# Two numbers in a kernel's planner: how many buffers stay reserved for elder requests

## The chip, the cores and the metric

The kernel runs on one core of a Trainium2 chip. A core has a matrix engine (TensorE, in the profile PE, with PEld for its weight loads), a vector engine (VectorE, DVE), a scalar engine (ScalarE, ACT), a general engine (GpSimd, POOL) and a sync engine (SP), which here only starts DMA transfers. Each works through its own list of instructions in order, and they wait for each other through semaphores. Working data lies in SBUF; matmul results go to PSUM, which has eight banks. The metric is the device time of one execution in microseconds (us), lower is better.

## The reference

The reference is one decoder block on a sequence of 2048 tokens of width 1024, in float32: a normalisation, one wide projection, two token mixers side by side (a gated linear recurrence and a chunked matrix memory with four heads), a merge with gates, an output projection, and a second normalisation with a residual.

```python
xn = rms_norm(x, g_pre)
proj = jnp.einsum("bsd,de->bse", xn, w_in)
...
u = causal_dwconv(r_x, rg_conv_w, rg_conv_b)
h_r = rg_lru(u, headwise(u, rg_w_a) + rg_b_a, headwise(u, rg_w_x) + rg_b_x, rg_lambda)
y_r = (h_r * jax.nn.silu(r_z.astype(jnp.float32))).astype(dt)
...
h_m = mlstm_chunkwise(q, k, v, i_pre, logf).transpose(0, 2, 1, 3)
...
y_m = (h_m * jax.nn.silu(m_z.astype(jnp.float32))).astype(dt)
y = jax.nn.sigmoid(gate_r) * jnp.einsum("bsr,rd->bsd", y_r, w_branch_r) + \
    jax.nn.sigmoid(gate_m) * jnp.einsum("bsm,md->bsd", y_m, w_branch_m)
out = jnp.einsum("bsd,de->bse", y, w_out)
return x + rms_norm(out, g_post)
```

## The kernel before

**Tiling and stages.** The 2048 tokens are four blocks of 512, taken in two passes (`sb` 0 and 1) of two blocks each. A pass is a phase A (projections and the recurrence) and a phase B (matrix memory, branch products, output). Nearly every working tile is 128 x 512 float32. To keep float32 accuracy, each matmul operand is split into a rounded high part and a low rest (`split`, `wsplit`): a cast on ACT (or DVE) and a subtraction on DVE. Each product is then three matmuls: high x high, high x low, low x high.

**Phase A.** It starts with the normalised input. `build_first` makes the tiles `a11` and `a12` from the first block; `build_second` makes `s1`, `s2`, `s3`, `s4` and `a22` from both blocks, since the projection of two blocks is done with seven products in place of eight (class `Pair`). Both call `token_scale`, which loads the rows of a block (`xh`), sums their squares, forms the factor of each token (`rsm`, `rstd`), puts it on a diagonal (`dg`, two buffers), and spreads it with a matmul `ones x dg` into one PSUM bank, four times, once per 128 tokens; the bank is copied out as `rb`. Everything that `build_second` makes is scaled with `rb`. In program order phase A records four calls of `ogate(0, h)`, which need only `a11` and `a12` and take four PSUM banks each (512 tokens by 256 columns), and then `build_second`, recorded under `nc.urgent(SPRI)`. Then come the pairs with their convolutions, gates and scans, and four calls of `ogate(1, h)`.

**Phase B.** Eight heads, u = 0 to 7: four of the first block, four of the second. A head loads its tiles (`mxr`, `cs`, `th`, `mz`), computes values and queries (`v`, `q`), scores (`s1`, `s2`), and then four `chunk` steps; each takes one bank for its output (`pt`) and two for the state update (`pc`), the last chunk of all only the first. Matmuls of other work are recorded between the heads: the branch products of the recurrence while u < 4 (their 16 inputs `yr` are held as 32 slots), the branch products of the memory for the first block while u is 4 or 5 (they make the 16 parts of `y`), and for u = 6 and 7 one `out_half` each, 96 matmuls of 512 columns on `y` into four banks, recorded after the four chunks of that head. After u = 7 come the branch products of the second block, during which the next pass's `build_first` is recorded, and the second block's output.

**The planner.** Nothing is issued while this program runs. Each call is recorded as an operation with its engine, an estimated cost, a place in program order (`seq`) and a priority (`pr`): the place less what `nc.urgent(n)` grants. `nc.early(n)` moves weight loads and splits 200 places up. `Plan.order` then plays the program through in estimated time: whenever an engine is free, it takes the available operation of lowest `pr`, unless it lies over `AHEAD` = 600 places behind the oldest operation not yet placed, or `can` says no. Each engine's instruction list is the order found. Since that is so, in the profile nearly every instruction has line 200 (the helper that issues a recorded operation) or 235 (its alternative on the other engine): they are told apart by tiles.

**Buffers.** A ring is a set of equal buffers: 78 slots of 128 x 512 in SBUF (tag `t`), eight PSUM banks (tag `ps`), six raw weight buffers (`raw`), four each of `whi` and `wlo`, and small ones. A tile takes a buffer of its ring when its first operation is placed and gives it back after its last. Requests of one ring are sorted by the program order of that first operation. `can(op)` decides whether `op` may take its buffers now:

```python
elder, q = 0, r[2]
while r[1][q] is not b:
    elder += id(r[1][q]) not in given
    q += 1
if r[0] <= min(elder, KEEP.get(b.tag, elder)):
    return False
```

Here `r[0]` is the number of free buffers and `elder` the number of requests that stand before this one in program order and haven't been served. With an empty `KEEP` the test is `r[0] <= elder`: a request is refused unless, after every elder one has been served, a buffer would still be free. The priority plays no part in it.

Of the kernel before, what the change touches and what calls it, by code (L numbers as in the profile page):

```python
# [125 lines left out]
class Plan:  # L126
# [133 lines left out]
    def order(self):  # L260
# [23 lines left out]
        def can(op):  # L284
            for b in op.allocs:
# [4 lines left out]
# [5 lines that stand above are left out]
# [1075 lines left out]
SPARE = 0  # L1370
VB = 1
SB = {}
KEEP = {}
AHEAD = 600
RAWB = 6
WPRI = 200
# [80 lines left out]
```

## Time and profile before

| | us |
|---|---|
| median of the 3 runs | 2010.14 |
| lowest and highest | 2008.55 and 2012.41 |
| the profiled execution, its time | 2010.83 |
| the profiled execution, its span from first to last instruction | 2009.1 |
| PE busy in it | 1969.2 (98%) |
| DVE busy | 1597.7 (80%) |
| ACT busy | 1142.2 (57%) |
| POOL busy | 517.2 (26%) |
| mean DMA rate | 156 GB/s |

The profile is of one execution. Its busy times are unions of an engine's instructions; matmuls overlap in the engine's pipeline, and their ends are modelled, so their starts are the safer reading. "Idle before" is the time in which an engine had nothing running before an instruction, put down to whatever ended that wait last. The granted clock is the share of full speed at which PE was allowed to run. The chain is followed back from the last instruction, at each step to what released it. Where 16 equal DMA engines are busy, the DMA share is their mean.

### The profile page before, as it was taken

Reading aid. Unit: us, or ns where it says so; the run is one execution under the profiler, and the core shown is the slowest. Engines: PE = TensorE matmul, PEld = TensorE weight load, DVE = VectorE, ACT = ScalarE, POOL = GpSimd, SP = SyncE. Lnnn points to the kernel's source line nnn. Section 1 sums busy time; section 2 is a strip of 40 time slices with the busy share of each in tenths; the row PEclk is TensorE's granted clock in tenths of the full one; section 3 lists DMA queues with packets and bytes.
Section 4 is the critical chain, followed back from the end, with each engine's and each line's share of the span. In section 5 each row is a group of like instructions: output and inputs, shape, how many; then the busy total and the mean of one; then the engine's idle time right before and its main releaser. Section 6 shows DMA issues by size and latency. Waiting matters only on the chain.

```text
span 2009.1 us, 30231 instructions
## 1 busy us (share of the span) xinstructions
PE 1969.2 (98%) x10240; PEld 1685.6 (84%) x10240; DVE 1597.7 (80%) x3026; ACT 1142.2 (57%) x2110; POOL 517.2 (26%) x864
## 2 busy tenths in 40 slices
PE   8999999999999999999999999999999999999998
PEld 8788888888898888887897788888888988888886
DVE  5998786978867889987559878879788677899783
ACT  5585664857555545644346757557585554465441
POOL 2444342343312111102033343432343111110010
PEclk9999999999999999999999999999999999999999
DMA  7224243242486466557471242413326754655562
GB/s 247 88 75 156 85 157 111 79 142 77 148 288 210 165 206 207 190 175 251 148 247 64 74 147 79 149 67 126 116 84 225 265 168 151 227 189 201 177 204 85
DMA packets 160988, 313.80 MB, mean 156 GB/s; under 512 B 19744, under 2 KB 40480, under 8 KB 160832
## 3 DMA queue, kind: packets, MB, share of 16 engines
q1 hardware_dynamic: 133440, 223.53, 33.9%
q0 software_dynamic: 27104, 88.21, 11.3%
q8 instruction: 80, 1.31, 0.3%
q14 instruction: 76, 0.62, 0.1%
q10 hardware_dynamic: 288, 0.13, 0.0%
HBM read 226.82 MB, written 84.97 MB: 155 GB/s over the span
## 4 chain that ended last, share of the span: by engine, by line
PE 95%; DVE 3%; ACT 1%; DMA 1%; issue 0%; SPq 0%; POOLq 0%; POOL 0%; ACTq 0%; DVEq 0%
PE ps L200 95%; DVE wlo L200 0%; DMA xh<-in_x_dram 0%; DVE kl L200 0%; DVE ql L200 0%; DMA xr<-in_x_dram 0%; DVE q L200 0%; DVE a L200 0%; ACT whi L200 0%; DVE mbc L200 0%; DVE cst L200 0%; DVE yml L200 0%; DVE th L200 0%; DVE cs L200 0%; ACT mbc L200 0%
## 5 line engine op out<-in xcount | busy, mean ns | idle before, releaser
L200 ACT CAST whi<-raw 128x512 fp32r<-128x512 f32 (+1 forms) x515 | 319.0, 621 | 544.9 <-PE ps L200 447.8
L200 DVE TENSOR_TENSOR wlo<-raw,whi 128x512 fp32r<-128x512 f32 (+1 forms) x576 | 394.0, 686 | 180.0 <-ACT whi L200 170.5
L200 DVE SCALAR_TENSOR_TENSOR u<-xq,vecs,u 128x511 f32<-128x511 f32 (+2 forms) x192 | 142.8, 746 | 9.5 <-ACT u L200 8.0
L200 DVE TENSOR_TENSOR raw<-raw,raw 128x512 f32<-128x512 f32 (+1 forms) x208 | 142.3, 686 | 2.7 <-DMA raw<-in_w_mo_dram 0.9
L200 POOL TENSOR_SCALAR h<-halo,vecs 128x2 f32<-128x2 f32 (+1 forms) x128 | 107.5, 853 | 1.5
L200 PE MATMUL ps<-ymh,whi 128*128 128x512 f32 x256 | 98.8, 395 | 2.7 <-ACT ymh L200 2.0
L200 PE MATMUL ps<-yrh,whi 128*128 128x512 f32 x256 | 100.8, 395 | 0.0
L200 PE MATMUL ps<-yml,whi 128*128 128x512 f32 x256 | 100.1, 392 | 0.7 <-DVE yml L200 0.7
L200 PE MATMUL ps<-yrl,whi 128*128 128x512 f32 x256 | 100.2, 391 | 0.0
L200 PE MATMUL ps<-yrh,wlo 128*128 128x512 f32 x256 | 100.0, 391 | 0.0
L200 PE MATMUL ps<-ymh,wlo 128*128 128x512 f32 x256 | 99.8, 391 | 0.0
L200 ACT ACT_TABLE_LOAD x65 | 83.4, 1283 | 4.0 <-PEq L1445 1.7
L200 PE MATMUL ps<-s2h,whi 128*128 128x512 f32 x192 | 75.4, 393 | 6.0 <-ACT m L200 6.0
L200 POOL COPY halo<-xq 128x3 f32<-128x3 f32 x64 | 48.7, 761 | 122.3 <-DVE xq L200 117.4
L200 PE MATMUL ps<-a11h,whi 128*128 128x512 f32 x192 | 76.3, 397 | 1.1 <-ACT whi L200 1.1
L200 PE MATMUL ps<-a11h,wlo 128*128 128x512 f32 x192 | 75.7, 394 | 0.9 <-DVE wlo L200 0.9
L200 PE MATMUL ps<-whi,yh 128*128 128x512 f32 x192 | 75.0, 391 | 1.0 <-ACT dn L200 1.0
L200 PE MATMUL ps<-s3h,whi 128*128 128x512 f32 x192 | 75.1, 391 | 0.8 <-ACT v L200 0.8
L200 PE MATMUL ps<-a11l,whi 128*128 128x512 f32 x192 | 75.5, 393 | 0.0
L200 PE MATMUL ps<-s2h,wlo 128*128 128x512 f32 x192 | 75.4, 393 | 0.0
L200 PE MATMUL ps<-s2l,whi 128*128 128x512 f32 x192 | 75.2, 392 | 0.0
L200 PE MATMUL ps<-a12h,whi 128*128 128x512 f32 x192 | 74.9, 390 | 0.0
(327 smaller groups left out, 6405.5 us busy)
## 6 DMA issues: line engine op xcount, KB each, us to landing
raw<-in_w_ch_dram SPq DMA_DIRECT2D x288, 256.0 KB, 2.7
raw<-in_w_out_dram SPq DMA_DIRECT2D x64, 256.0 KB, 2.7
raw<-in_w_mo_dram SPq DMA_DIRECT2D x48, 256.0 KB, 5.7
xh<-in_x_dram SPq DMA_DIRECT2D x32, 256.0 KB, 5.3
dth<-th POOLq DMA_DIRECT2D x32, 256.0 KB, 3.7
dgr<-tg POOLq DMA_DIRECT2D x32, 256.0 KB, 3.0
dmx<-xq POOLq DMA_DIRECT2D x32, 256.0 KB, 2.5
dc<-u POOLq DMA_DIRECT2D x32, 256.0 KB, 2.5
```

Of the source, the lines that this page charges most:

```text
L200: getattr(eng.real, what)(*[real(v) for v in a], **{n: real(v) for n, v in kw.items()})
```

## The change

One constant of the planner changes. For PSUM banks the number of elder requests that must be provided for is capped at two, and for the 78 SBUF slots at ten: with at least three free banks, or at least eleven free slots, any request is granted, however many elder ones are still open. Where fewer elders are open than the cap, the test is as before. The other rings (`raw`, `whi`, `wlo` and the small ones) have no entry and keep the old test. The recorded program, its operations, priorities, engines' estimated costs and the look-ahead of 600 are the same; only the order in which operations are placed on the engines can differ, and with it which physical buffer a tile gets, and which of two engines takes a copy that may run on either.

```diff
 SPARE = 0
 VB = 1
 SB = {}
-KEEP = {}
+KEEP = {"ps": 2, "t": 10}
 AHEAD = 600
 RAWB = 6
 WPRI = 200
```

## The prediction

> **What bounds the kernel now.** I read the page's busy times first, then its chain that ended last.
>
> ```profile
> span 2009.1 us, 30231 instructions
> PE 1969.2 (98%) x10240; PEld 1685.6 (84%) x10240; DVE 1597.7 (80%) x3026; ACT 1142.2 (57%) x2110; POOL 517.2 (26%) x864
> ...
> PE 95%; DVE 3%; ACT 1%; DMA 1%; issue 0%; SPq 0%; POOLq 0%; POOL 0%; ACTq 0%; DVEq 0%
> ```
>
> TensorE (PE) is busy for 1969.2 of 2009.1 us and is 95% of the chain. The change alters no instruction's work, only the order, so what it can win is PE's idle time, 39.9 us in all, and the time that PE loses to a lower clock after it has idled. Where the idle time lies is read from the windows view: a stretch, its length, busy time (and count) of PE, PEld, DVE, ACT, POOL, then the granted clock, the DMA share and GB/s.
>
> ```profile
> 0.00:50.00 50.00, 43.05 (x307) 40.91 (x308) 27.12 (x72) 27.21 (x64) 13.67 (x29) 0.97 0.71 247
> 50.00:112.00 62.00, 56.93 (x302) 47.86 (x300) 58.35 (x99) 37.88 (x67) 31.71 (x26) 0.97 0.23 77
> 112.00:783.00 671.00, 671.00 (x3406) 572.86 (x3405) 543.06 (x1000) 406.48 (x715) 194.68 (x344) 1.00 0.44 153
> ...
> 839.00:855.00 16.00, 12.80 (x87) 10.92 (x87) 16.00 (x35) 9.71 (x23) 1.79 (x3) 1.00 0.68 220
> 855.00:889.00 34.00, 33.74 (x185) 28.94 (x184) 24.09 (x54) 15.61 (x36) 2.39 (x5) 1.00 0.50 172
> 889.00:898.00 9.00, 6.54 (x47) 5.90 (x47) 8.93 (x20) 5.94 (x13) 0.00 (x0) 1.00 0.84 281
> ...
> 937.00:945.00 8.00, 5.08 (x20) 3.14 (x19) 7.14 (x12) 5.24 (x9) 0.00 (x0) 1.00 0.46 158
> ...
> 1060.00:1112.00 52.00, 45.76 (x185) 35.78 (x184) 50.08 (x85) 32.63 (x55) 24.75 (x26) 0.93 0.18 61
> 1112.00:1832.00 720.00, 719.83 (x3711) 616.29 (x3710) 592.61 (x1114) 434.25 (x777) 195.94 (x342) 1.00 0.44 150
> 1832.00:1849.00 17.00, 14.06 (x86) 12.49 (x85) 17.00 (x34) 10.81 (x25) 2.15 (x5) 0.90 0.65 220
> ...
> 1883.00:1888.50 5.50, 4.65 (x27) 3.66 (x27) 5.50 (x12) 3.63 (x8) 0.00 (x0) 1.00 0.96 352
> ...
> 2000.90:2009.10 8.20, 0.00 (x0) 0.00 (x0) 2.31 (x4) 0.69 (x2) 1.13 (x2) 0.82 0.16 64
> ```
>
> Length less PE busy is the idle time. The two long stretches hold 0.0 and 0.17 us in 1391 us: there the order can only lose. The first 50 us (6.95) and the tail (8.20) wait for the first loads and the last output. What is left are two kinds of places. **Kind A**, the start of each phase A, 5.07 us in 50:112 and 6.24 in 1060:1112, with DVE busy 58.35 of 62 and 50.08 of 52. **Kind B**, the last two heads of each phase B: 3.20 (839:855), 2.46 (889:898), 2.94 (1832:1849) and 0.85 (1883:1888.5), 9.45 together, with DVE busy nearly all the time. And 2.92 in 937:945, between them. So PE idles where DVE is full; the question is whether DVE was idle before, or PE had other work that the planner withheld.
>
> **Kind A: the scaling matmul that waits for sixteen banks.** The timeline of the second site, then the start of the first:
>
> ```profile
> 1025.60 0.28 DVE L200 TENSOR_SCALAR dg<-ident,rstd 128x128 f32<-128x128 f32 x1
> ...
> 1027.97 0.21 DVE L200 TENSOR_SCALAR rsm<-ss 128x1 f32<-128x1 f32 x1 [0.82 <-ACT xh L200]
> ...
> 1046.90 0.61 PE L200 MATMUL ps<-dg,ones 128*128 128x128 f32 x4
> ...
> 1047.39 0.51 DVE L200 TENSOR_SCALAR dg<-ident,rstd 128x128 f32<-128x128 f32 x2 [0.39 <-PE ps L200]
> ...
> 1048.82 0.59 ACT L200 COPY rb<-ps 128x512 f32<-128x512 f32 x1 [0.18 <-PE ps L200]
> ...
> 1049.44 0.75 DVE L200 SCALAR_TENSOR_TENSOR a<-a,vecs,rb 128x512 f32<-128x512 f32 x1 [1.54 <-ACT rb L200]
> ```
> ```profile
> 30.68 0.30 DVE L200 TENSOR_SCALAR dg<-ident,rstd 128x128 f32<-128x128 f32 x1
> ...
> 51.66 0.51 DVE L200 TENSOR_SCALAR dg<-ident,rstd 128x128 f32<-128x128 f32 x2 [0.39 <-PE ps L200]
> ```
>
> `dg` is ready at 1025.60, but the matmul that reads it runs at 1046.90; `rb`, on which all of build_second hangs, comes at 1048.82. That matmul has the highest priority of all (`urgent(BPRI)`, 1000), its input is there, and PE runs younger-priority matmuls meanwhile. Only `can` refuses it: its bank comes, in program order, behind the 4 x 4 = 16 banks of four `ogate` calls, and the old rule demands more free banks than elders not yet served. The first site shows the same 21 us between the second dg (30.68) and the third (51.66). What DVE did in the gap, by groups of lines, busy, mean ns, idle before:
>
> ```profile
> L200 DVE TENSOR_TENSOR wlo<-raw,whi 128x512 fp32r<-128x512 f32 x7 | 4.8, 692 | 14.0 <-ACT whi L200 14.0
> ```
> ```profile
> L200 DVE TENSOR_TENSOR wlo<-raw,whi 128x512 fp32r<-128x512 f32 x9 | 6.2, 692 | 10.4 <-ACT whi L200 10.3
> ```
>
> From 1029 to 1046.9 DVE idles 14.0 us, from 32 to 51 10.4 us, just ahead of the stretches in which it is full. With the new rule 3 free banks suffice. One ogate holds 4 of 8; the one before is evacuated soon after its last matmul, so 3 are free at some point of each ogate. I put rb about 19 us earlier: last rsm at 1027.97, plus what lies between the dg at 1047.39 and rb's end at 1049.41, 2.0 us, so about 1030. build_second has 44 full-width DVE operations; the chain's spacing of 0.6 us makes that 27 us, and a half fits into 14.0. Its s2 split, the 24th, was late by this much:
>
> ```profile
> 76.35 0.50 PE L200 MATMUL ps<-s2h,whi 128*128 128x512 f32 x1 [3.00 <-ACT m L200]
> ...
> 78.03 0.63 PE L200 MATMUL ps<-s2h,whi 128*128 128x512 f32 x1
> 78.46 0.63 PE L200 MATMUL ps<-s2l,whi 128*128 128x512 f32 x1
> ```
> ```profile
> 1072.09 0.50 PE L200 MATMUL ps<-s2h,whi 128*128 128x512 f32 x1 [3.00 <-ACT m L200]
> ```
> ```profile
> PE ps L200 <- DVE ul L200: 2.4, 2, 1.4
> ```
>
> 24 x 0.6 = 14.4 us from 1030 has it done by about 1049 beside the weights, 20 us ahead of use. The two 3.00 us waits go, and so should the short ones behind them. The 2.4 us for `ul` are the recurrence's own chain (convolution, split, gate) and stay. Kind A: 5.07 + 6.24 - 2.4 = **8.9 us**; bounds 0 and 11.3.
>
> **Kind B: out_half behind the chunks' banks.**
>
> ```profile
> 838.79 0.68 DVE L200 TENSOR_TENSOR yl<-tgl,yh 128x512 fp32r<-128x512 f32 x1
> ...
> 841.36 1.29 DVE L200 TENSOR_TENSOR wlo<-raw,whi 128x512 fp32r<-128x512 f32 x2
> ```
> ```profile
> 846.49 0.39 PE L200 MATMUL ps<-vh,kh 128*128 128x258 f32 x1 [1.66 <-ACT kh L200]
> ...
> 855.00 0.28 PE L200 MATMUL ps<-vh,kl 128*128 128x258 f32 x1
> 855.12 0.49 PE L200 MATMUL ps<-whi,yh 128*128 128x512 f32 x1
> ```
> ```profile
> 891.86 0.39 PE L200 MATMUL ps<-vh,wth 128*128 128x258 f32 x1 [1.36 <-ACT wth L200]
> ...
> 897.26 0.28 PE L200 MATMUL ps<-vh,kl 128*128 128x258 f32 x1
> 897.38 0.39 PE L200 MATMUL ps<-whi,yh 128*128 128x512 f32 x1
> ```
>
> The last part of y is split at 839.5 and two weights by 842.6, yet out_half starts at 855.12, straight behind the last of the four chunks' bank requests (12: one `pt` and two `pc` each), and again at 897.38. Between, PE waits for DVE with 96 ready matmuls of about 0.23 us (855.12 to 855.45 and on) withheld. The new rule lets out_half take banks down to two, and its matmuls fill the waits; DVE has 10 us free in 855:889 for what it then still owes. I take two thirds of 9.45, **6.3 us**, since a list made ahead won't meet every short wait; bounds 0 and 9.45.
>
> **The clock.** After the wait of 3.00 us the matmuls come 0.43 us apart (78.03 to 78.46), not 0.23. Granted clock times busy time gives 0.03 x 56.93 + 0.07 x 45.76 + 0.10 x 14.06 = 6.3 us lost in the three disturbed stretches. Half, **3.1 us**, should go with the waits. The Trainium skill, page "TensorE: Matmul & The Clock Gate", section "HAM oscillation — how this bites in real kernels", gives the rule "no PE-idle gaps >~3.4µs". By it gaps of 3.00 us and less would cost no clock, this term were 0 and the sum 3.1 us higher; the rows here show the slow matmuls all the same, so I keep it.
>
> **Slots.** With `"t": 10` a younger request needs at most 11 free of 78. It lets loads and splits run earlier: the 2.92 us of 937:945 might shrink (0 to 2.9; I take 0). Against it, younger tiles can eat what an elder head needs at once: eb, four k, two wt, four q halves, 11 slots, over the ten kept. Each DMA moved earlier also sits on SP ahead of weight loads behind it. The nearest row for such a stall is the 1.36 us wait above. Two of them are **2.7 us** lost; the far ends are none, and one in each of 16 heads, 22 us.
>
> **Sum.** 8.9 + 6.3 + 3.1 - 2.7 = 15.6 us. The profiled execution took 2010.83 us (span 2009.1 and 1.7 around it), 0.7 over the median of the three runs. 2010.8 - 15.6 gives 1995.2; I say **1995 us**. The bounds of its terms: everything goes and nothing is lost, 11.3 + 9.45 + 6.3 + 2.9 = 30, 1981; kind A alone, less the two stalls, 6, 2005.
>
> **Rivals.**
> 1. *Half of it.* DVE's 1597.7 us stay, and its queue is only shifted: the waits come back at the next needy place (gates, 937:945). For it speaks that DVE is 81% busy even in the long stretch (543.06 of 671); against it the 14.0 and 10.4 us of measured idle time. Half of 15.6: 2003 us. Chance 0.15.
> 2. *Nothing moves.* Another limit holds the same operations: the look-ahead of 600 (AHEAD), or the rings of weights, which keep the old rule. For out_half the weights are in place; the dg matmuls stand behind four ogates of 114 recorded operations and some 30 more, about 490, within the 600. So mostly against: 2010 us. Chance 0.11.
> 3. *Slower: slots run short in phase B.* While u < 4 the 32 slots of yr are held all along, and the early loads of the next head go in as soon as 11 are free. If a head then finds its eleven tiles one short, PE stalls by about 1.36 us per head; it decides against the change from about 13 heads on (13 x 1.36 = 18 against 18.3 won). With nearly all of 16 and kind B's gain lost too, 2010.8 - 12 + 22 = 2021 us. For it speaks that the two long stretches are full now and have nothing to win; against it that elder requests still go first whenever they are ready, and DVE has a fifth free. Chance 0.17.
> 4. *Slower by the clock.* If banks taken early leave PE many short idles, the granted clock of the long stretches could fall from 1.00 to the 0.97 seen in 50:112: 0.03 x 1391 = 42 us, 2036 us with the gains. No idle time there supports it. Chance 0.02. The Trainium skill's same page, section "A second HAM failure mode: psum-queue depth-cycling", tells of such oscillation; the trace shows none here.
>
> **How the numbers follow.** The forecast has 0.55, with its own range 1983 to 2004. Faster by over 0.2% (4 us, about what a measurement of this kernel tells from no change): forecast and rival 1, 0.70. Same: rival 2, 0.11. Slower: rivals 3 and 4, 0.19. Cases of one sign hold most, so there is one range, 1982 to 2013: it leaves out a little below, and most of rivals 3 and 4, some 0.18 in all.
>
> **What would show it.** Right: in the new trace the second pair of dg follows the first within some 5 us at both sites; rb near 34 and 1030; the DVE gaps filled; no 3.00 us wait before s2h; `ps<-whi,yh` starts before the head's last `vh,kh`, and the granted clock of 1060:1112 near 1.00. Wrong: dg still 20 us apart; out_half still behind the chunks; or PE idle time in the long stretches, ended by tiles that DVE or ACT wrote late, or by `tgl`, `cs` or `mxr` loads.

## The result, and the profile after

| | before | after |
|---|---|---|
| median, us | 2009.35 (2008.53 to 2012.41) | 1977.06 (1975.61 to 1977.79) |
| profiled execution, its time | 2010.83 | 1975.61 |
| its span | 2009.1 | 1973.8 |

The ratio is 0.9836, with a 95% interval of 0.9819 to 0.9853: 32.3 us faster. The forecast was 1995 us, with a range from 1982: the direction was right, the size was not, and the time lies below the range. The page of the changed kernel, span, busy times and the chain that ended last by engine:

```profile
span 1973.8 us, 30190 instructions
...
PE 1955.6 (99%) x10240; PEld 1679.8 (85%) x10240; DVE 1600.5 (81%) x3052; ACT 1158.6 (59%) x2108; POOL 551.0 (28%) x864
...
PE 96%; DVE 1%; POOL 1%; DMA 1%; issue 1%; ACT 0%; SPq 0%; POOLq 0%; ACTq 0%; DVEq 0%
```

PE issues the same 10240 matmuls. Its idle time fell from 39.9 to 18.2 us, but its **busy** time fell too, from 1969.2 to 1955.6, though no matmul went away. Of the 35.3 us that the span lost, 13.6 lay where the page says busy. The windows view (stretch, length, then busy time and count of PE, PEld, DVE, ACT, POOL, granted clock, DMA share, GB/s) answers to the stretches shown of before; all of phase B lies some us earlier now:

```profile
50.00:112.00 62.00, 60.89 (x325) 52.36 (x324) 56.96 (x104) 41.67 (x70) 36.70 (x37) 1.00 0.25 88
112.00:783.00 671.00, 671.00 (x3416) 572.76 (x3415) 542.19 (x1007) 406.58 (x712) 201.54 (x333) 1.00 0.44 154
820.00:860.00 40.00, 40.00 (x239) 35.34 (x238) 38.46 (x91) 23.47 (x49) 3.18 (x8) 1.00 0.58 188
860.00:900.00 40.00, 39.62 (x232) 34.47 (x231) 34.41 (x84) 22.89 (x56) 6.21 (x8) 1.00 0.88 307
900.00:945.00 45.00, 44.06 (x197) 35.85 (x197) 42.09 (x71) 21.09 (x40) 8.06 (x14) 1.00 0.63 212
1040.00:1092.00 52.00, 51.55 (x242) 42.97 (x241) 49.03 (x84) 36.29 (x57) 36.91 (x32) 1.00 0.20 71
1092.00:1790.00 698.00, 698.00 (x3592) 596.95 (x3592) 574.32 (x1083) 430.94 (x753) 202.91 (x338) 1.00 0.44 153
1790.00:1840.00 50.00, 50.00 (x290) 43.82 (x289) 46.47 (x108) 29.17 (x65) 4.87 (x9) 1.00 0.65 222
1840.00:1900.00 60.00, 59.52 (x314) 50.49 (x313) 44.20 (x91) 24.15 (x51) 10.28 (x17) 1.00 0.57 195
```

The two long stretches are as full as before (671.00 of 671.00 and 698.00 of 698.00), and no stretch here has a clock under 1.00. The places of kind A idle 1.11 and 0.45 us, those of kind B under half a us each. Who PE still waits for, in total, times, longest:

```profile
PE ps L200 <- DMA ident<-in_ident_dram: 3.9, 1, 3.9
PE ps L200 <- ACT uh L200: 1.6, 2, 1.1
```

and the same list of before, four rows that have no successor:

```profile
PE ps L200 <- ACT m L200: 6.0, 2, 3.0
...
PE ps L200 <- ACT kh L200: 4.0, 2, 2.4
...
PE ps L200 <- ACT ymh L200: 2.0, 1, 2.0
...
PE ps L200 <- ACT wth L200: 1.8, 3, 1.4
```

`ident`, the first load, leads now, and `uh`, the recurrence's own chain, is the longest wait in mid-kernel. The steps, in the timeline (start, duration, engine, operation, idle before it):

```profile
32.18 0.28 DVE L200 TENSOR_SCALAR dg<-ident,rstd 128x128 f32<-128x128 f32 x1
32.70 0.29 DVE L200 TENSOR_SCALAR dg<-ident,rstd 128x128 f32<-128x128 f32 x1 [0.24 <-POOL rstd L200]
...
34.12 0.59 ACT L200 COPY rb<-ps 128x512 f32<-128x512 f32 x1 [1.14 <-PE ps L200]
...
72.47 0.39 PE L200 MATMUL ps<-s2h,whi 128*128 128x512 f32 x1
...
837.19 0.47 PE L200 MATMUL ps<-whi,yh 128*128 128x512 f32 x1
...
1008.31 0.28 DVE L200 TENSOR_SCALAR dg<-ident,rstd 128x128 f32<-128x128 f32 x1
...
1011.48 0.29 DVE L200 TENSOR_SCALAR dg<-ident,rstd 128x128 f32<-128x128 f32 x1 [0.58 <-POOL rstd L200]
...
1012.81 0.32 DVE L200 TENSOR_SCALAR dg<-ident,rstd 128x128 f32<-128x128 f32 x1
...
1051.63 0.39 PE L200 MATMUL ps<-s2h,whi 128*128 128x512 f32 x1
```

The third and fourth `dg` stand within 3 us of the second (29.92) at the first site and within 5 us at the other. `rb` comes at 34.1 and, in the second pass, at 1014.2, which is 19 and 35 us earlier than before; of the 35, 17 come from the `dg` before it, which is itself that much earlier. In the gap, 32 to 51 us, DVE is now busy for 18.36 us (8.18 before). The first `s2h` matmuls (72.47, 1051.63) have no wait before them, and out_half starts at 837.19, ahead of that head's last `ps<-vh,kh` (851.41). Every step that was named as a sign is there. So the question is one of size.

**A finer measure.** Where a matmul waits, the modelled end of the one before it (0.39 us long, 0.23 apart) hides part of the wait, and half clock counts as busy. So for the table below each distance between the starts of two successive matmuls has the median distance of its shape before taken off (0.227 us at 512 columns, 0.120 at 256 and 258). What is left, summed, is **lost PE time**: 57.9 us before and 22.9 after, which is 35.1 less before rounding, against 35.3 of the span. By places: **A**, 50 to 150 and 1050 to 1150 us; **B**, 800 to 900 and 1750 to 1950; and **hand-over**, 900 to 950, where the last `ym` of a pass are loaded and split and the next input is made (the 937:945 of the prediction). The rest, 13 to 17 us, is much the same in all kernels. The places are read from one execution of each kernel, whose time lies within 1.7 us of the median, in e4 3.0 us below it.

| kernel | median, us | ratio, 95% interval | A | B | hand-over |
|---|---|---|---|---|---|
| before | 2009.35 | | 18.8 | 20.4 | 4.2 |
| after | 1977.06 | 0.9819 to 0.9853 | 2.1 | 4.0 | 1.5 |
| e3, scaling bank alone | 1992.54 | 0.9901 to 0.9930 | 1.1 | 20.9 | 3.1 |
| e4, out_half's banks alone | 2001.26 | 0.9942 to 0.9971 | 15.9 | 4.2 | 11.8 |
| e5, these five banks | 1984.68 | 0.9860 to 0.9889 | 1.9 | 3.5 | 10.1 |
| e1, all banks, no slots | 1985.16 | 0.9863 to 0.9896 | 3.3 | 3.5 | 10.6 |
| e2, slots, no banks | 1996.86 | 0.9924 to 0.9954 | 10.7 | 16.7 | 2.0 |
| e6, all but the scaling bank | 1985.28 | 0.9858 to 0.9891 | 10.5 | 4.8 | 1.5 |
| e7, all but out_half's banks | 1990.27 | 0.9882 to 0.9912 | 2.5 | 16.6 | 2.1 |
| e11, three banks kept back | 1977.84 | 0.9821 to 0.9851 | 2.6 | 7.2 | 0.9 |
| e8, four banks kept back | 1982.11 | 0.9842 to 0.9871 | 0.7 | 10.0 | 1.4 |
| e12, twenty slots kept back | 1986.74 | 0.9862 to 0.9895 | 2.7 | 4.2 | 10.7 |
| e13, banks, and slots for build_first | 1976.53 | 0.9821 to 0.9851 | 3.1 | 6.1 | 1.2 |
| e14, all but build_first's slots | 1979.36 | 0.9834 to 0.9863 | 2.2 | 3.1 | 4.9 |
| e18, e1 with build_first earlier | 1984.10 | 0.9858 to 0.9891 | 3.5 | 3.5 | 8.0 |
| e17, e1 with build_first later | 1982.63 | 0.9855 to 0.9884 | 2.7 | 4.0 | 7.8 |

### The profile page after: what moved, and what is told of

The parts are those of the page before. It is cut to its first block, busy times and chain, and to the rows that moved or that the text cites. A ratio compares the mean times of both kernels' runs of the same rounds, so it can differ in the third digit from the quotient of the medians.

```text
span 1973.8 us, 30190 instructions
## 1 busy us (share of the span) xinstructions
PE 1955.6 (99%) x10240; PEld 1679.8 (85%) x10240; DVE 1600.5 (81%) x3052; ACT 1158.6 (59%) x2108; POOL 551.0 (28%) x864
## 3 DMA queue, kind: packets, MB, share of 16 engines
q1 hardware_dynamic: 133440, 223.53, 34.1%
## 4 chain that ended last, share of the span: by engine, by line
PE 96%; DVE 1%; POOL 1%; DMA 1%; issue 1%; ACT 0%; SPq 0%; POOLq 0%; ACTq 0%; DVEq 0%
PE ps L200 96%; POOL hc L200 1%; DVE wlo L200 0%; DMA xh<-in_x_dram 0%; DMA dth<-th 0%; DMA gp<-in_gpost_dram 0%; DVE o L200 0%; DVE u L200 0%; DMA dym<-mz 0%; DVE th L200 0%; POOL out_dram L200 0%; POOL rstd L200 0%; POOL r L200 0%; DVE a22l L200 0%; ACT uh L200 0%
## 5 line engine op out<-in xcount | busy, mean ns | idle before, releaser
L200 ACT CAST whi<-raw 128x512 fp32r<-128x512 f32 (+1 forms) x484 | 300.2, 621 | 469.7 <-PE ps L200 367.0
L200 POOL TENSOR_SCALAR hc<-halo,vecs 128x3 f32<-128x3 f32 x64 | 81.6, 1275 | 8.1 <-DVE u L200 6.0
L200 POOL TENSOR_TENSOR rstd<-rsm,eps_t 128x1 f32<-128x1 f32 x32 | 20.2, 634 | 200.8 <-DVE rsm L200 186.1
L200 PE MATMUL ps<-wlo,yh 128*128 128x512 f32 x192 | 75.1, 391 | 0.0
L200 PE MATMUL ps<-whi,yl 128*128 128x512 f32 x192 | 74.9, 391 | 0.0
L200 PE MATMUL ps<-s3h,wlo 128*128 128x512 f32 x192 | 74.7, 389 | 0.0
```

What stands on the lines that cost most here:

```text
L200: getattr(eng.real, what)(*[real(v) for v in a], **{n: real(v) for n, v in kw.items()})
```

## The experiments

**The two numbers apart (e1, e2).**

```diff
-KEEP = {}
+KEEP = {"ps": 2}      # e1
+KEEP = {"t": 10}      # e2
```

> Only the bank half of the change: KEEP = {"ps": 2}, slots as before. Theory (the banks carry the gain): 1975 to 1982 us, no half-clock window after the first 50 us, PE idle time 18 to 21 us. Rival (the slots carry a good part, since loads and splits for the next head and the next input can start earlier): 1985 us or more, with the wait at 937 to 945 of the kernel before still there.

> Only the slot half: KEEP = {"t": 10}, banks as before. Theory: 2004 to 2012 us, the second pair of dg still some 20 us behind the first at both starts of a phase A, out_half still behind the chunks. Rival (slots carry a good part): 1990 to 2000 us. The prediction's third rival (slots run short in phase B): over 2013 us, with PE waits inside the long stretches.

Banks alone win 24.6 us, slots alone 12.9, both 32.3. That the slots win anything was against the forecast. They win at different places: with the banks alone A and B are cured and the hand-over gets worse, from 4.2 to 10.6; with the slots alone the hand-over is cured, A halved, and B barely touched. How the slots halve A stays open: in e2 `rb` comes as late as before (52.63 and 1042.36) and DVE is as idle from 32 to 51 us (8.74 us busy), yet both waits of 3.0 us for `m` are gone. PE's waits in e1, first row:

```profile
PE ps L200 <- ACT ymh L200: 5.8, 1, 5.8
```

**The banks, one request at a time (e3, e4, e5).** One buffer can be given a cap of its own, while all others keep the old test:

```diff
-                if r[0] <= min(elder, KEEP.get(b.tag, elder)):
+                if r[0] <= min(elder, KEEP.get(b.tag, elder) if b.keep is None else b.keep):
...
-        ps = psum()                         # token_scale, e3 and e5
+        ps = psum(2)
...
-        pt = [psum() for _ in range(NT)]    # out_half, e4 and e5
+        pt = [psum(2) for _ in range(NT)]
```

> KEEP is empty, and only the bank of token_scale is granted with three free banks: kind A of the prediction alone. The starts of the matmuls say that PE lost about 16.7 us more at the two kind A places before than after (distances between starts less the usual distance of each shape). Theory (the loss is to be read from matmul starts, and all of it goes): 1990 to 1995 us. Rival (the prediction's sizes, 8.9 us of idle time and some 2 of clock): 1997 to 2001 us. If kind A isn't held by that one bank: 2009 us.

> KEEP is empty, and only the four banks of each out_half are granted with three free banks: kind B of the prediction alone. Theory: 1990 to 1998 us, the waits in the last two heads of both phases B gone; the wait at 937 to 945 may stay, as it comes after out_half. Rival (the prediction's size, 6.3 us and some clock): 2001 to 2004 us. If out_half isn't held by its banks: 2009 us.

> KEEP is empty; the bank of token_scale and the four banks of out_half are granted with three free banks, all other banks as before. Theory (these five banks are the whole of the bank half): the time of the bank half alone, 1983 to 1987 us, which is also what the two single parts add up to (2009.8 - 17.2 - 8.5 = 1984). Rival (other banks, such as those of the pairs or the chunks, gain too): clearly above, 1989 us or more.

The edit stands in the two helpers, so it holds for every call: build_first's scaling matmul has the cap too, and so has the second block's out_half. The one bank of the scaling matmul wins 17.2 us. In the windows of e3 both places of kind A are at full clock, the first is full, and the second idles 1.01 us:

```profile
50.00:112.00 62.00, 62.00 (x333) 53.87 (x332) 55.79 (x99) 42.53 (x75) 35.88 (x36) 1.00 0.25 85
...
1040.00:1092.00 52.00, 50.99 (x275) 44.07 (x275) 47.11 (x79) 31.76 (x59) 33.38 (x26) 1.00 0.26 84
```

out_half's four banks win 8.5 by themselves, and 16.2 us of lost time at B, half of which is given back at the hand-over. (That 16.2 less 7.6 comes out near 8.5 is partly luck: the profiled execution was 12.6 us faster than that of before, 3 us of it at A, and it lacks two of the half-clock stretches of before, near 16 and 1108 us.) (In the kernels with a cap per buffer line 200 has become 201, and 235 has become 236.) PE's waits in e4, and what DVE does meanwhile:

```profile
PE ps L201 <- DVE ymh L236: 8.1, 1, 8.1
```
```profile
927.89 2.08 DVE L201 SCALAR_TENSOR_TENSOR a<-a,vecs,rb 128x512 f32<-128x512 f32 x3
929.88 1.89 DVE L201 TENSOR_TENSOR a11l<-a,a11h 128x512 fp32r<-128x512 f32 x3
931.68 2.07 DVE L201 SCALAR_TENSOR_TENSOR a<-a,vecs,rb 128x512 f32<-128x512 f32 x3
933.67 0.69 DVE L201 TENSOR_TENSOR a11l<-a,a11h 128x512 fp32r<-128x512 f32 x1
934.27 1.29 DVE L201 TENSOR_TENSOR a12l<-a,a12h 128x512 fp32r<-128x512 f32 x2
935.48 1.41 DVE L201 SCALAR_TENSOR_TENSOR a<-a,vecs,rb 128x512 f32<-128x512 f32 x2
936.80 0.42 DVE L236 CAST ymh<-ym 128x512 fp32r<-128x512 f32 x1
```

The next pass's input (`a`, `a11l`, `a12l`) fills DVE without a break from 927.9, and the cast of `ym` that PE stands still for comes behind it, in the order of the list; both last loads of `ym` had landed by 932.2. Both edits together (e5) give 25.2 us, about their sum of 25.7, and the time of e1: these five banks are the whole of the banks' half.

**Undoing one of them in the full change (e6, e7).** The same edit, the other way round: `psum(99)` in one place, so that this request alone keeps the old test.

> The changed kernel with the bank of token_scale alone under the old rule (more free banks than elders), all else as changed. Theory: kind A comes back as far as the slot half doesn't cover it; in the slot half alone the matmul starts show 5.4 + 5.4 us lost at the two places against 1.5 + 0.6 after the change, so 8 to 11 us more than the changed kernel, 1985 to 1988 us. Rival (with earlier slots the bank no longer matters): 1977 us.

> The whole change, but the four banks of out_half keep the old test. Theory (these banks are what freed the places of kind B): the matmuls of out_half come again behind the chunks' banks. With the slots alone the matmul starts of 800 to 850 us and of 1800 to 1850 us still lost 5.1 us each, so about 10 us come back: 1985 to 1989 us. Rival (the slots alone would have filled DVE in time, so the banks don't matter any more once they are there): 1977 to 1980 us, and out_half starts late without PE waiting.

Without the scaling bank 8.2 us come back, without out_half's banks 13.2. A comes back only by half (10.5 of 18.8): the slots alone had halved it too. B comes back for the most part (16.6 of 20.4), and out_half starts at 850.6 instead of 837.2; the time lies 1.3 us above the expected span.

**How many to keep back (e8, e11, e12).** `KEEP` with `"ps"` 4 or 3, or with `"t"` 20.

> Banks kept back: four in place of two; slots as in the change. Theory: an ogate holds four of the eight banks nearly all the time, so five free banks hardly occur while ogates run, the scaling matmul is refused as under the old test, and the second pair of dg comes near 51 and 1035 us again: about the 8 us of the run without that bank's grant, 1984 to 1988 us (a little more if out_half is refused too). Rival (any cap is enough, since five banks are free for a moment between two ogates): 1977 to 1979 us, dg near 30 us.

> Banks kept back: three in place of two. Theory: four free banks do occur beside an ogate that holds four, once the one before it is evacuated, so the scaling matmul is granted somewhat later than with two (dg and rb by a few us) and the time is that of the change, 1976 to 1980 us. Rival (the four are never all free while ogates run): as with four kept back, 1984 to 1988 us.

> Slots kept back: twenty in place of ten; banks as in the change. Theory 1 (the slots' part needs only that some loads of the hand-over go earlier, for which 21 free of 78 are enough part of the time): 1977 to 1980 us. Theory 2 (the slots are nearly all taken there, and each ten kept back delays the next input's loads): between the change and the banks alone, 1980 to 1985 us, with the first xh load of the second pass later than 870 us and a longer wait for ymh near 930 us.

Three is as good as two. Four costs 5 us, and not where it was expected: five banks are free often enough for the scaling matmul. Timeline of e8:

```profile
31.75 0.30 DVE L200 TENSOR_SCALAR dg<-ident,rstd 128x128 f32<-128x128 f32 x1
...
34.01 0.28 DVE L200 TENSOR_SCALAR dg<-ident,rstd 128x128 f32<-128x128 f32 x1
```

The loss is at B (10.0). out_half's first matmul comes as early as in the change (835.20), but its matmuls break off and go on at 848.96, and the chunks' matmuls between have waits again. That out_half asks for four banks in a row and gets the later ones late is the likely reason; no run tested it. Twenty slots lose the whole gain of the slots, with a wait of 5.75 us for `ymh` as in e1; the time lies 1.7 us above the expected span.

**Where the slots win (e13, e14, e18, e17).** In e13 the cap of ten slots holds only for the tiles made in build_first, in e14 for all but these. In e18 and e17 build_first is recorded elsewhere and the slots keep the old test.

```diff
+        v.buf.keep = slots[0]      # in t2k; slots[0] is set only inside build_first
...
-KEEP = {}
+KEEP = {"ps": 2}               # e13, slots[0] = 10
+KEEP = {"ps": 2, "t": 10}      # e14, slots[0] = 999
...
-XAT = 2
+XAT = 0                        # e18, with KEEP = {"ps": 2}
+XAT = 5                        # e17, with KEEP = {"ps": 2}
```

> The bank half (KEEP = {"ps": 2}), and the slot cap of ten only for the tiles made inside build_first (xh, rb, the a tiles and their splits). Theory (what the slots win on top of the banks is the next pass's input, whose 24 DVE operations stand in front of the last ym splits in the two bank-only kernels): 1976 to 1979 us, the wait before the first matmul on the last ymh, 5.8 us in the bank half alone, under 1 us. Rival (heads' loads or others carry it): 1983 to 1986 us.

> The changed kernel with the tiles made inside build_first under the old slot rule. Theory: 1983 to 1987 us, as the bank half alone, with a wait of some 5 us before the matmul on the last ymh. Rival (heads' loads or others carry the slots' part): 1976 to 1979 us.

> The banks' half of the change alone (slots under the old test), and the next input's build_first recorded two branch products earlier in program order (XAT 0 in place of 2). Theory (what the slots bought is that the next input's loads and its rb come earlier, so that build_first's DVE operations no longer stand between rb and the last splits of ym): fewer elder requests stand before it, its xh loads move up under the old test too, rb comes before 915 us (922.2 with the banks alone), PE's wait for ymh falls from 5.8 to under 3 us and the half clock behind it goes: 1976 to 1981 us. Rival (the slots helped somewhere else, and the hand-over only shows it): the wait may shift, but the time stays at 1984 to 1987 us.

> The banks' half alone, and build_first recorded three branch products later (XAT 5 in place of 2). Theory: rb comes no earlier than 922 us, and 13 of build_first's DVE operations in place of 15 still stand ahead of the last yml in DVE's list, so the wait for ymh stays near 5 us: 1983 to 1987 us. Rival (recording it later puts the splits of ym first and is as good as giving it slots early): 1976 to 1981 us with a wait under 3 us.

build_first's slots suffice (1976.5), but are hardly needed: the 1979.4 of e14 lie under what was expected of it. And an early `rb` is not what counts: in e18 it comes at 906.0 instead of 922.2, but the time stays at 1984, as the rival had it, with 4.4 us of waiting for `ymh`. Recorded later (e17), the time is 1982.6, 0.4 us under what the theory gave, with waits of up to 3.1 us in place of one near 5. The timeline of e18 shows why, DVE first, then ACT:

```profile
917.40 1.41 DVE L200 SCALAR_TENSOR_TENSOR o<-o,rstd,xr 128x512 f32<-128x512 f32 x2
...
919.92 2.07 DVE L200 SCALAR_TENSOR_TENSOR a<-a,vecs,rb 128x512 f32<-128x512 f32 x3
921.91 1.89 DVE L200 TENSOR_TENSOR a11l<-a,a11h 128x512 fp32r<-128x512 f32 x3
...
924.32 2.07 DVE L200 SCALAR_TENSOR_TENSOR a<-a,vecs,rb 128x512 f32<-128x512 f32 x3
926.31 1.89 DVE L200 TENSOR_TENSOR a12l<-a,a12h 128x512 fp32r<-128x512 f32 x3
928.12 0.74 DVE L200 SCALAR_TENSOR_TENSOR a<-a,vecs,rb 128x512 f32<-128x512 f32 x1
...
930.15 1.29 DVE L200 TENSOR_TENSOR yml<-ym,ymh 128x512 fp32r<-128x512 f32 x2
```
```profile
928.89 0.62 ACT L200 CAST a12h<-a 128x512 fp32r<-128x512 f32 x1 [1.85 <-DVE a L200]
929.42 1.14 ACT L200 CAST ymh<-ym 128x512 fp32r<-128x512 f32 x2
```

PE waits for the cast `ymh`, here on ACT. It stands in ACT's list behind casts of `a`, and these wait for DVE. With an early `rb` (e18) 15 of build_first's 16 operations of `a`, `a11l` and `a12l` stand between the last output operation (`o`) and the last split of `ym`, without it (e1) all 16.

Part of such a wait is the load of `ym` itself, which is issued late. In e1 the earlier of the last two loads lands at 924.64, half a microsecond after PE fell idle, and its cast starts at 929.22, so some 4.6 of the 5.8 us are the order of the lists. In e17 that load takes 8.4 us, lands at 926.21, and is cast at 927.08: there half of the longest wait of 3.1 us is the load.

In the changed kernel half of the 16 have gone ahead of the output operations. Two rows from either side of those, same view:

```profile
900.41 2.08 DVE L200 SCALAR_TENSOR_TENSOR a<-a,vecs,rb 128x512 f32<-128x512 f32 x3 [0.60 <-ACT rb L200]
...
918.97 1.41 DVE L200 SCALAR_TENSOR_TENSOR o<-o,rstd,xr 128x512 f32<-128x512 f32 x2
...
927.10 0.68 DVE L200 TENSOR_TENSOR yml<-ym,ymh 128x512 fp32r<-128x512 f32 x1
```

Counted in the traces in this way, over all kernels:

| operations of build_first in between | kernels (the rest of the 16: before `o`, or after `ym`) | lost at the hand-over, us |
|---|---|---|
| 4 to 8 | after, e7, e11, e13 (8 to 12 before) | 0.9 to 2.1 |
| 9 to 11 | before, e2, e3, e6, e8, e14 (5 to 7 after) | 1.4 to 4.9 |
| 13 | e17 (3 after) | 7.8 |
| 15 or 16 | e1, e4, e5, e12, e18 (one before at most) | 8.0 to 11.8 |

So the loss goes roughly with that count. It isn't the whole account: at about the same count e8 (10) loses 1.4 us and e14 (11) 4.9, and the loads of `ym` play a part. There are two ways to a low one: slots early, so that half the work goes ahead, or slots late, so that a third of it is left for afterwards, as in e14. Both are read from the traces; no run moved these operations alone and left everything else in place, and which other early slots push them back in e14 was not tried.

## Why the prediction was right in direction and wrong in size

**The mechanisms** were all there: the scaling matmul was held by the bank test alone (e3, e6), out_half likewise (e4, e7), and DVE had the room. Rival 1 (half) and rival 2 (nothing) fall with the time; but what rival 1 said, that waits come back at 937:945, is what the banks alone do (e1, e4). Rival 3 (slots short in phase B) falls with 671.00 and 698.00 busy in the two long stretches, rival 4 with their clock of 1.00.

**The pool was mis-measured.** The prediction's pool was PE's idle time and the granted clock, 39.9 and 6.3 us, and its bound for "everything goes" 30. The time went below that bound, because a wait costs more than its idle time on the page: of the 57.9 us lost before, 24.3 lie between matmuls with no visible gap, and 14.9 of the 22.9 after. Half clock is about 6 of the 9.4 us that went there. Most of the rest, some 3 us, was lost by matmuls within 1.5 us behind a wait (4.9 us before, 2.0 after). Where there was a gap, 25.6 us went, of which 21.5 were visible.

**Kind A, 8.9 us and half of its clock loss (2.5): measured 17.2** (e3). Visible idle time fell by 10.3 (5.07 + 6.24 to 0.00 + 1.01) instead of 8.9. Half clock, which by matmul starts had cost 1.2 + 1.65 + 1.65 = 4.5 us here, went whole. Some 3 us (17.7 of lost time less these two) had been hidden. The 2.4 us kept back for the recurrence's own chain were kept back rightly in part: in the changed kernel 1.6 us stand there as a wait for `uh`.

**Kind B, 6.3 us: measured 8.5 in time** (e4), and 16.2 of lost time at its own places. "Two thirds" was too low, since the list made ahead does meet the short waits; over 800 to 900 and 1750 to 1950 the idle time of 10.4 us falls to 0.9 in the changed kernel. And the term lacked what follows: whatever moves the last matmuls up moves the hand-over's deadline up too, and the hand-over grew by 7.6 us. The prediction asked what is late next only in its first rival, and put nothing of it into this term.

**Clock, 3.1 us: measured about 6.** The rows (distance of the matmuls doubled after a 3.00 us wait) were right and the half was too cautious: all four stretches of half clock in the middle of the kernel are gone. (Where the prediction sets this term to 0, the sum of what is won would be 3.1 us lower and the time 3.1 us higher; it says that the sum would be higher.)

**Slots, -2.7 us: measured +8.1** (1985.16 to 1977.06). This is the step with the wrong sign. The two stalls of 1.36 us didn't come: the two long stretches stayed full, and no head's tiles are among PE's waits in the changed kernel. What the term had wrong is the 2.92 us of 937:945, taken as 0: they were the tip of a place that the banks' half raises to 10.6, and the slots take it back to 1.5. How they do it is known by place (e13) and by the count above, not by a run that moves these operations alone. By themselves the slots win 12.9, most of it at A, where the banks win too; so the two halves together (32.3) give less than their sum (37.5).

With the measured terms the sum is 17.2 + 8.5 + 8.1 = 33.8 us, against 32.3 measured. Of the 18.2 us between this sum and the forecast's 15.6, the slots are 10.8, kind A with its share of the clock some 6, kind B with its share some 1.5: the wrong sign of the slots is the largest error.

## What to carry to other kernels

A buffer test that protects program order can hold back the very operation that has the highest priority; where an operation with its inputs ready runs 20 us late beside an engine with free time, look at what it must allocate, not at its priority. Price a wait by the starts of the instructions around it, clock included, and not by the idle time on the page. And when a term moves work up, ask at once which deadline it moves up with it: here the banks alone make the hand-over lose 6.4 us more, and the slots pay that back.

## What the runs showed of the hardware

Half clock follows waits well under 3 us. Windows of PE before (length, PE busy, granted clock, DMA share, GB/s):

```profile
1100.00:1107.90 7.90, 6.53 (x28) 1.00 0.01 2
1108.40:1111.70 3.30, 3.30 (x8) 0.51 0.00 0
...
1838.00:1842.30 4.30, 1.87 (x13) 1.00 0.82 283
1842.30:1846.70 4.40, 4.40 (x23) 0.61 0.66 195
```

1.37 us of waiting (7.90 less 6.53) came ahead of the first, 2.43 us ahead of the second, and PE then ran at half speed for some 3.4 us, about 1.6 us lost each time. The Trainium skill's page "TensorE: Matmul & The Clock Gate", section "HAM oscillation — how this bites in real kernels", warns only of idle gaps over some 3.4 us; this trace doesn't agree, since the gaps here are 1.37 and about 2.4 us long. Nor does every such wait cost clock: the 1.1 us for `uh` in the changed kernel leaves its stretch at 1.00. After a longer wait at the hand-over the slow stretch can be longer: by the clock records of the traces it lasts 3.41 us with the wait of 3.1 us (e17), 6.83 with 4.4 (e18), and 10.24 with 5.8 and with 8.1 (e1, e4), part of it while PE still waits. Windows of e1, behind its 5.8 us for `ymh`:

```profile
933.00:936.00 3.00, 3.00 (x8) 0.50 0.00 0
936.00:939.00 3.00, 3.00 (x12) 0.80 0.00 0
939.00:945.00 6.00, 6.00 (x28) 1.00 0.60 180
```

The matmuls reach their usual pace, 14 in 3 us, only behind 939. The stretch loses 10.6 us in all, of which 5.8 show as this wait.
